# Two transformer blocks on one core: the first stage in half rows, and buffer classes that begin at multiples of 1 KB

## The chip, the cores and the metric

The kernel runs on one core of a Trainium2 chip. The metric is the device time of one execution in microseconds (us). Before the change it is 1069.44 us, the median of three runs (1069.07 to 1070.16).

## The reference

512 rows of 1,024 numbers in fp32 go through two blocks.

- **Block 1.** `h = rms_norm(x, norm_g)`; `proj = h @ w_in`, split into the q, k, v and gate z of a differential attention with four heads, and the q, six k/v streams, gate z and mixing gates of a sparse attention that adds a compressed, a selected and a window branch. `x = x + concat(o_diff, o_nsa) @ w_out`.
- **Block 2.** `h = rms_norm(x, g_mix)`; `proj = h @ w_in_2`, split for a short causal convolution, an attention over the 128 best keys by an index score with a relative bias (`rel_bias`, 32 buckets by 8 heads), and two gates; `x = x + merged @ w_out_2`. Then `x = x + (silu(h2 @ w_ffn_gate) * (h2 @ w_ffn_up)) @ w_ffn_down` with 2,816 inner columns, and a last rms_norm.

Block 1 starts with the function that matters at the start of the kernel:

```python
def rms_norm(x, g):
    xf = x.astype(jnp.float32)
    r = lax.rsqrt(jnp.mean(xf * xf, axis=-1, keepdims=True) + RMS_EPS)
    return (xf * r).astype(x.dtype) * g
```

## The kernel before

**Products.** An fp32 product is made of three fp32r matmuls. Each operand is a pair, hi (the value rounded to fp32r) and lo (the rest), and `mm3` issues hi·hi, hi·lo and lo·hi into one PSUM bank. In each matmul one operand is loaded as weights (the stationary one, 128 x 128) and the other streams past (the moving one, 256 to 512 columns). In the trace's names `acc<-whi,hT` is moving `whi`, stationary `hT`; the last name is the stationary one. Three generators write the dense products: `gen_ii` keeps activations (`hT`) stationary and moves the weights in units of 256 to 320 columns; `gen_i` keeps weights stationary and moves all 512 rows; `gen_tt` moves weights of 512 columns. The gate and up products of the feed-forward part go in pairs by a scheme with seven block products (class `Pair`, L1277 to L1345); their stationary operand is the weight (`wh`, `wl`) and their moving one `hA` with 256 columns.

**Weights.** `_load` (L195) issues the DMA of a unit of weights on SP's queue, `_split` makes the pair: ACT casts (L206, `whi`), DVE or POOL subtracts (L208, `wlo`).

**Buffers.** All tiles in SBUF come from classes of equal buffers that are used in turn: `k8` (13 of 8,192 B per partition), `k4` (13 of 4,096 B), `kf` (3 of 4,096 B), `k2` (19 of 2,048 B), `sm` (28 of 96 B). A constant (`K.const`) is a class of its own. The classes are laid out in the order of their first use. By their sizes, behind a scratch area of 4,096 B that the program has anyway and four constants of 32 B, `kf` and `k4` begin at byte 4,224 (128 beyond a multiple of 1,024) and `k2` at 69,760 (128 beyond one). `mhalf`, `identF`, `sm`, `identR` and `ones` follow with 3,776 B, so that `k8` begins at 112,448 (832 beyond a multiple of 1,024, 320 beyond one of 512). `hT`, `hA`, `act`, `mg`, `qk` and `oTd` stand in `k8`; raw weights, `whi`, `wlo`, `wh` and `wl` in `k4`, with one exception: `split_of` (L1264) puts the pair of weights of some first blocks, `early`, into one `k8` buffer, under the name `wh`.

**The first stage** (L423 to L467, L1452 to L1467). The rows of `x` come as four row tiles of 128, each by two DMAs of 512 columns. Meanwhile `norm_g` is spread over the partitions: eight numbers of each partition's row are transposed (`grow`, `gT`), then broadcast and transposed back into `gB1`, whose first half DVE copies and whose second ACT. TensorE runs 6 transposes of `identF` into `warm` ahead of `grow`, and 12 more are written behind the copies. Then, row tile by row tile, `rms_rows` (L371) squares and sums both halves (ACT; the second half of the first tile DVE, L377), POOL adds and takes the power -0.5 (L383, L384), DVE scales the halves (L385, L389, `xn`), and `put_hT` (L395) transposes each half by four transposes, casts (ACT, `hT` hi) and subtracts (DVE, `hT` lo). After each row tile but the first `K.step()` issues a step of the first dense product, `dk0`. `relative_rows` (L523) loads `rel_bias` transposed into `rbT`; `constants` (L478) loads the small vectors (`gv`, `vrow`, `lmb`).

**The order.** Within an engine the instructions stand in the order of a scheduler that runs over the program with times of its own; so a row in the program may be issued ahead of an earlier one. The queues of DMA are set by the same pass.

## Time and profile before

| what | value |
|---|---|
| median of three runs | 1069.44 us (1069.07 to 1070.16) |
| profiled execution | 1070.19 us, of which the span of the trace is 1068.4 us |
| mean granted clock of TensorE, share of full speed | 0.994 |
| busy time of PE (matmul) | 1043.4 us, 98% of the span, 7,257 instructions |
| busy time of DVE, ACT, POOL | 720.0, 556.2 and 396.8 us |
| DMA | 109.69 MB, mean 103 GB/s |

The profile names TensorE PE, VectorE DVE, ScalarE ACT and GpSimd POOL. The span is what the trace covers; the profiled execution lasted 1.8 us longer than it. A time in the timeline is counted from the start of the span. The end of a matmul is modelled, and matmuls are pipelined, so the time that one more matmul costs is not its duration but the distance from its start to the next start: a row of n matmuls that lasts T has a spacing of (T minus the duration of one) over n minus 1.

### The profile page before, as it was taken

To read this page: it belongs to the slowest core of one execution; us is meant where nothing else is said; L and a number is where in the kernel's file an instruction comes from. 1 tells how busy PE (TensorE), PEld (TensorE's weight loads), DVE (VectorE), ACT (ScalarE), POOL (GpSimd) and SP (SyncE) were. 2 spreads that over 40 slices of the span, in tenths; PEclk is the share of its full clock that TensorE was granted. 3 is DMA by queue.
4 is the path that set the end of the run, shared out by engine and by line. 5 is a ranking of instruction groups with operands and counts; after the bars stand their busy time and mean duration, and the time that the engine had idled before them with its cause. 6 is when DMAs were issued, how large, how long until landed. Compare 5 with 4: busy or idle time off the path is not lost.

```text
span 1068.4 us, 18973 instructions
## 1 busy us (share of the span) xinstructions
PE 1043.4 (98%) x7257; PEld 962.7 (90%) x7257; DVE 720.0 (67%) x1468; ACT 556.2 (52%) x1155; POOL 396.8 (37%) x403
## 2 busy tenths in 40 slices
PE   6999999999999999999999999999999999999997
PEld 6999898899779899888888888989999999999995
DVE  5787467446994646999423653979987777777724
ACT  5476678647884445632323776436544444444433
POOL 3442357466367322112115875920012112121241
PEclk8999999999999999999999999999999999999999
DMA  5344421221114435335322323641433323333122
GB/s 167 114 138 136 102 62 41 58 82 60 57 43 129 140 92 167 100 98 155 112 79 69 90 70 108 237 139 60 158 109 119 117 82 100 94 114 109 31 90 79
DMA packets 128085, 109.69 MB, mean 103 GB/s; under 512 B 20393, under 2 KB 119154, under 8 KB 127994
## 3 DMA queue, kind: packets, MB, share of 16 engines
q1 hardware_dynamic: 126906, 105.83, 32.6%
q0 software_dynamic: 1072, 2.65, 0.7%
q8 instruction: 57, 0.93, 0.4%
q14 instruction: 34, 0.28, 0.1%
q10 hardware_dynamic: 16, 0.00, 0.0%
HBM read 103.13 MB, written 6.84 MB: 103 GB/s over the span
## 4 chain that ended last, share of the span: by engine, by line
PE 90%; DVE 4%; POOL 2%; ACT 2%; issue 1%; DMA 0%; SPq 0%; POOLq 0%; DVEq 0%; ACTq 0%
PE acc L164 76%; PE pt L178 5%; PE sc L164 4%; PE o L164 4%; POOL wlo L208 1%; ACT p L636 1%; DVE p L634 1%; DVE acc L1513 0%; POOL mg L1213 0%; DVE mg L1216 0%; PE warm L178 0%; DMA gv<-in_diff_k_norm_g 0%; ACT junk L380 0%; DVE PTa L653 0%; ACT whi L206 0%
## 5 line engine op out<-in xcount | busy, mean ns | idle before, releaser
L208 POOL TENSOR_TENSOR wlo<-raw,whi 128x1024 fp32r<-128x1024 f32 (+4 forms) x99 | 205.0, 2075 | 444.4 <-ACT whi L206 365.5
L164 PE MATMUL acc<-hA,wh 128*128 128x256 f32 x1264 | 218.0, 279 | 0.7 <-ACT wh L1272 0.7
L206 ACT CAST whi<-raw 128x1024 fp32r<-128x1024 f32 (+4 forms) x143 | 132.0, 924 | 125.1 <-PE acc L164 80.1
L164 PE MATMUL acc<-hT,whi 128*128 128x512 f32 x608 | 194.5, 398 | 0.0
L164 PEld LDWEIGHTS acc<-hA,wh 128*128 128x128 f32 x1264 | 189.0, 189 | 1.3 <-ACT wh L1272 0.9
L164 PE MATMUL acc<-whi,hT 128*128 128x256 f32 (+3 forms) x896 | 180.7, 290 | 1.0 <-DVE hT L402 1.0
L164 PE MATMUL acc<-hA,wl 128*128 128x256 f32 x584 | 162.4, 278 | 0.0
L164 PEld LDWEIGHTS acc<-whi,hT 128*128 128x128 f32 x896 | 144.1, 189 | 1.7 <-DVE hT L402 1.2
L164 PEld LDWEIGHTS acc<-hT,whi 128*128 128x128 f32 x608 | 112.2, 188 | 24.5 <-ACT r L1512 0.2
L164 PE MATMUL acc<-whi,act 128*128 128x256 f32 (+1 forms) x640 | 130.0, 289 | 0.0
L164 PE MATMUL acc<-wlo,hT 128*128 128x256 f32 (+3 forms) x448 | 128.6, 288 | 0.0
L164 PE MATMUL acc<-hT,wlo 128*128 128x512 f32 x304 | 120.9, 398 | 0.0
L164 PEld LDWEIGHTS acc<-hA,wl 128*128 128x128 f32 x584 | 109.6, 188 | 0.0
L164 PEld LDWEIGHTS acc<-whi,act 128*128 128x128 f32 x640 | 103.9, 188 | 2.5
L164 PE MATMUL acc<-wlo,act 128*128 128x256 f32 (+1 forms) x320 | 92.3, 289 | 0.0
L636 ACT ACTIVATE p<-p,s 128x128 f32<-128x128 f32 (+3 forms) x128 | 72.2, 565 | 29.9 <-DVE s L634 27.1
L164 PEld LDWEIGHTS acc<-wlo,hT 128*128 128x128 f32 x448 | 84.4, 189 | 0.4
L1272 ACT CAST wh<-raw 128x1024 fp32r<-128x1024 f32 x55 | 57.6, 1052 | 50.1 <-PE acc L164 43.6
L1273 DVE TENSOR_TENSOR wl<-raw,wh 128x1024 fp32r<-128x1024 f32 x51 | 63.3, 1245 | 29.8 <-PE acc L164 17.3
L208 DVE TENSOR_TENSOR wlo<-raw,whi 128x1024 fp32r<-128x1024 f32 (+5 forms) x44 | 53.6, 1221 | 42.3 <-ACT whi L206 42.2
L164 PEld LDWEIGHTS acc<-hT,wlo 128*128 128x128 f32 x304 | 57.2, 188 | 13.1
L164 PEld LDWEIGHTS acc<-wlo,act 128*128 128x128 f32 x320 | 60.1, 188 | 1.3
(279 smaller groups left out, 2044.4 us busy)
## 6 DMA issues: line engine op xcount, KB each, us to landing
raw<-in_w_in SPq DMA_DIRECT2D x52, 512.0 KB, 3.6
raw<-in_w_ffn_gate SPq DMA_DIRECT2D x28, 512.0 KB, 3.6
raw<-in_w_ffn_up SPq DMA_DIRECT2D x22, 512.0 KB, 4.6
raw<-in_w_ffn_down SPq DMA_DIRECT2D x36, 256.0 KB, 5.2
raw<-in_w_out SPq DMA_DIRECT2D x16, 512.0 KB, 3.3
raw<-in_cmp_w SPq DMA_DIRECT2D x8, 512.0 KB, 3.6
raw<-in_w_in SPq DMA_DIRECT2D x10, 384.0 KB, 3.4
rel_all<-rel_rows POOLq DMA_DIRECT2D x1, 2560.0 KB, 18.0
```

Source lines behind the costliest of these rows:

```text
L164: self.nc.tensor.matmul(out, lhsT, rhs, start=start, stop=stop, skip_group_check=True)
L178: self.nc.tensor.transpose(out, in_, ident)
L206: self.nc.scalar.copy(hi, raw)
L208: (self.nc.gpsimd if every and self.split and self.split % every == 0 else self.nc.vector).tensor_tensor(lo, raw, hi.bitcast(F32), op=OP.s ...
L634: V.tensor_tensor_reduce(out=p[:, :n], in0=sc[:, :n], in1=bias, scale=-scale, scalar=3e38, op0=OP.add, op1=OP.min, accum_out=nm)
L636: S["exp"] = A.activation(p[:, :n], p[:, :n], AF.Exp, scale=-1.0, bias=nm, accum_out=z).ins
L1272: A.copy(hi, src)
L1273: eng.tensor_tensor(lo, src, f32(hi), op=OP.subtract)
```

## The change

- The warming transposes are 6 and 6 in place of 6 and 12, and the last 6 move `gB1` past `identF`, where the 12 moved nothing that anything else writes.
- Six constants (`identF` 512 B, `KC` 256 B, `mhalf`, `ones`, `rowok`, `c01` of 32 B each: 896 B) are made ahead of all else. With the 4,096 B and the four constants of before they make 5,120 B, so that `kf`, `k4` (from 5,120 on), `k2` (70,656) and `k8` (109,568, taken ahead of the other constants since `new_hT()` is called early) all begin at multiples of 1,024 B.
- Both halves of `gB1` are copied by ACT.
- The loop over row tiles is `first_rows`: for each tile the sums (the second half on DVE for the first two tiles), then scaling and transposing of half 0, then scaling of half 1, then transposing of half 1 of the tile before. `K.step()` follows every tile, the first too.
- The DMA of `rbT` is issued after the last one of `x`.

```diff
-WARM = 6, 12
+WARM = 6, 6
...
+    identF, KC = K.const([P, P], "identF"), K.const([P, 64], "KC")
+    mhalf, ones, rowok = [K.const([P, 1], name) for name in ("mhalf", "ones", "rowok")]
+    c01 = K.const([P, 2], "c01")
     xin = [t("kf" if tt < 3 else "k4", [P, D], F32, "xt") for tt in range(NT)]
...
     x_load(0)
-
-    mhalf = K.const([P, 1], "mhalf")
+    S["hT"] = new_hT()
+
     V.memset(mhalf, -0.5)
-    identF = K.const([P, P], "identF")
...
-        copy((V, A)[b], gB1[:, b * T:(b + 1) * T], pt.rearrange("p a b -> p (a b)"))
-    for _ in range(WARM[1]):
-        K.tr(warm, identF, identF)
+        A.copy(gB1[:, b * T:(b + 1) * T], pt.rearrange("p a b -> p (a b)"))
+    for b in range(WARM[1]):
+        K.tr(warm, gB1[:, b * P:(b + 1) * P], identF)
...
-        nc.sync.dma_start(rbT, h["rel_bias_2"].rearrange("b h -> h b"))
+        with tc.issue_after(S["x"]):
+            nc.sync.dma_start(rbT, h["rel_bias_2"].rearrange("b h -> h b"))
...
+    def first_rows():
+
+        rs, xn = {}, {}
+
+        def stats(tt):
+            ss, r = sm(2), sm(1)
+            for c in range(2):
+                a, junk = xin[tt][:, c * T:(c + 1) * T], t("k2", [P, T], F32, "junk")
+                if c and tt < 2:
+                    V.tensor_tensor_reduce(out=junk, in0=a, in1=a, scale=1.0 / 1024.0, scalar=0.0, op0=OP.mult,
+                                           op1=OP.add, accum_out=ss[:, c:c + 1])
+                else:
+                    A.activation(junk, a, AF.Square, scale=1.0 / 32.0, accum_out=ss[:, c:c + 1])
+            G.tensor_scalar(r, ss[:, 0:1], ss[:, 1:2], EPS, op0=OP.add, op1=OP.add)
+            G.tensor_tensor(r, r, mhalf, op=OP.pow)
+            rs[tt] = r
+
+        def norm(tt, b):
+            a = slice(b * T, (b + 1) * T)
+            xn[tt, b] = t("k2", [P, T], F32, "xn")
+            V.scalar_tensor_tensor(xn[tt, b], xin[tt][:, a], rs[tt], gB1[:, a], op0=OP.mult, op1=OP.mult)
+
+        def put(tt, b):
+            pt = ps([P, 4, P], name="pt")
+            for k in range(4):
+                K.tr(pt[:, k, :], xn[tt, b][:, k * P:(k + 1) * P], identF)
+            s = slice(tt * P, (tt + 1) * P)
+            A.copy(S["hT"][0][b][:, :, s], pt)
+            V.tensor_sub(S["hT"][1][b][:, :, s], pt, f32(S["hT"][0][b][:, :, s]))
+            tick()
+
+        for tt in range(NT):
+            stats(tt)
+            norm(tt, 0)
+            put(tt, 0)
+            if tt == 0:
+                K._split()
+            norm(tt, 1)
+            if tt:
+                put(tt - 1, 1)
+            K.step()
+        put(NT - 1, 1)
...
-    for tt in range(NT):
-        halves = [xin[tt][:, 0:T], xin[tt][:, T:D]]
-        xn = rms_rows(halves, gB1, BOTH, tt == 0)
-        if tt == 0:
-            K._split()
-        put_hT(xn, tt, S["hT"])
-        if tt:
-            K.step()
+    first_rows()
```

On PE, at the start of the program, the order before is this (`pt<-identF,s` are the transposes that make `gB1`):

```order
L178 MATMUL warm<-identF 128x128 x18
L178 MATMUL pt<-identF,grow 128x8
L178 MATMUL pt<-identF,s 128x128 x8
L178 MATMUL pt<-identF,xn 128x128 x16
L164 MATMUL acc<-whi,hT 128x256
L164 MATMUL acc<-wlo,hT 128x256
```

and with the change:

```order
L178 MATMUL warm<-identF 128x128 x6
L178 MATMUL pt<-identF,grow 128x8
L178 MATMUL pt<-identF,s 128x128 x8
L178 MATMUL warm<-identF,gB 128x128 x4
L178 MATMUL pt<-identF,xn 128x128 x4
L178 MATMUL warm<-identF,gB 128x128 x2
L164 MATMUL acc<-whi,hT 128x256
L164 MATMUL acc<-wlo,hT 128x256
```

All 18 warming transposes stood ahead of `grow`, also the 12 written behind it; now 6 do, and the first matmul of `dk0` stands behind 4 transposes of `xn` in place of 16 (12 matmuls later there is a row of 16).

On DVE, from the copy of `gT` on, before:

```order
L447 COPY s<-pt 128x8
L377 ISA junk,s<-xt 128x512
L377 ISA s 128x1
L277 COPY gB<-pt 128x512
L385 SCALAR_TENSOR_TENSOR xn<-xt,s,gB 128x512
L389 SCALAR_TENSOR_TENSOR xn<-xt,s,gB 128x512
L402 TENSOR_TENSOR hT<-pt,hT 128x4x128 x2
L208 TENSOR_TENSOR wlo<-raw,whi 128x1024
```

and with the change, up to the last scaling and the `GD` constant (made of `gv`):

```order
L1470 SCALAR_TENSOR_TENSOR xn<-xt,s,gB 128x512 x2
L1478 TENSOR_TENSOR hT<-pt,hT 128x4x128
L1459 ISA junk,s<-xt 128x512
L1459 ISA s 128x1
L208 TENSOR_TENSOR wlo<-raw,whi 128x1024
L1470 SCALAR_TENSOR_TENSOR xn<-xt,s,gB 128x512 x2
L208 TENSOR_TENSOR wlo<-raw,whi 128x1024
L1470 SCALAR_TENSOR_TENSOR xn<-xt,s,gB 128x512 x2
L208 TENSOR_TENSOR wlo<-raw,whi 128x840
L1470 SCALAR_TENSOR_TENSOR xn<-xt,s,gB 128x512 x2
L1478 TENSOR_TENSOR hT<-pt,hT 128x4x128 x6
L504 TENSOR_TENSOR GD<-gv 128x64
```

The copy of `gB` is gone from DVE, one subtraction for `hT` stands ahead of the first `wlo` in place of two, and six of the eight stand in a row behind all scalings.

On SP's queue the first rows before are:

```order
L429 DMA xt<-in_x 128x512 x2
L525 DMA rbT<-in_rel_bias 8x32x1
L195 DMA raw<-in_w_in 128x4x256
L429 DMA xt<-in_x 128x512 x2
L195 DMA raw<-in_w_in 128x4x256
```

and with the change:

```order
L433 DMA xt<-in_x 128x512 x2
L195 DMA raw<-in_w_in 128x4x256
L433 DMA xt<-in_x 128x512 x2
L195 DMA raw<-in_w_in 128x4x256
L433 DMA xt<-in_x 128x512 x4
```

`rbT` has left its place behind the first tile of `x` and stands behind the loads of the first weights and of `cmp_w2`.

## Rows read from the trace of the kernel before

**Rows 1.** The chain that ended last, shares of the span by engine.
```profile
PE 90%; DVE 4%; POOL 2%; ACT 2%; issue 1%; DMA 0%; SPq 0%; POOLq 0%; DVEq 0%; ACTq 0%
```

**Rows 2.** Windows: us, busy PE, PEld, DVE, ACT, POOL, PEclk, DMA share, GB/s.
```profile
5.00:10.00 5.00, 3.29 (x21) 2.77 (x19) 2.88 (x6) 1.02 (x2) 0.88 (x2) 0.84 1.01 358
10.00:15.00 5.00, 0.38 (x2) 0.00 (x0) 2.94 (x4) 4.73 (x11) 1.27 (x2) 0.50 1.09 318
15.00:20.00 5.00, 4.53 (x27) 4.53 (x28) 4.24 (x7) 3.44 (x9) 3.79 (x6) 0.64 0.08 19
```

**Rows 3.** Timeline of PE, first stage: start, us, engine, line, operation, idle before and releaser.
```profile
1.69 3.77 PE L178 MATMUL warm<-identF 128*128 128x128 f32 x18 [1.69 <-POOL identF masks.py:199]
...
8.42 1.97 PE L178 MATMUL pt<-identF,xn 128*128 128x128 f32 x8 [1.46 <-DVE xn L385]
15.47 1.97 PE L178 MATMUL pt<-identF,xn 128*128 128x128 f32 x8 [5.09 <-DVE xn L385]
17.09 0.56 PE L164 MATMUL acc<-whi,hT 128*128 128x256 f32 x1
...
32.39 0.29 PE L164 MATMUL acc<-wlo,hT 128*128 128x280 f32 x1
```

**Rows 4.** Timeline of DVE and ACT, first stage.
```profile
5.65 0.17 DVE L447 COPY s<-pt 128x8 f32<-128x8 f32 x1 [4.11 <-PE pt L178]
5.74 0.68 DVE L377 CUSTOM_DVE_ANT_0 junk<-xt 128x512 f32<-128x512 f32 x1
7.61 0.75 DVE L385 SCALAR_TENSOR_TENSOR xn<-xt,s,gB 128x512 f32<-128x512 f32 x1 [0.36 <-POOL s L384]
12.59 1.22 DVE L208 TENSOR_TENSOR wlo<-raw,whi 128x1024 fp32r<-128x1024 f32 x1 [0.86 <-ACT whi L206]
...
11.53 1.03 ACT L206 CAST whi<-raw 128x1024 fp32r<-128x1024 f32 x1
```

**Rows 5.** Timeline of POOL and DVE around the constant GD, and PE's wait there.
```profile
25.30 2.00 POOL L208 TENSOR_TENSOR wlo<-raw,whi 128x840 fp32r<-128x840 f32 x1 [4.81 <-ACT whi L206]
25.40 1.98 DVE L506 TENSOR_TENSOR GD<-gv 128x64 f32<-128x64 f32 x1 [1.33 <-DMA gv<-in_diff_k_norm_g]
PE acc L164 <- DVE hT L402: 1.0, 1, 1.0
```

**Rows 6.** What the DMA engines moved in each us from 0 to 40.
```profile
GB/s 0 35 307 208 151 268 360 377 390 395 391 369 316 276 238 92 3 0 0 0 3 13 38 31 94 64 40 39 148 288 325 74 0 76 320 129 0 0 16 0
```

**Rows 7.** Timeline of PE: the first feed-forward products, weights and `hA` both in `k8`.
```profile
717.46 5.92 PE L164 MATMUL acc<-hA,wh 128*128 128x256 f32 x48
...
725.32 6.00 PE L164 MATMUL acc<-hA,wh 128*128 128x256 f32 x48
```

**Rows 8.** Timeline of PE: later feed-forward products, weights in `k4`.
```profile
736.06 0.39 PE L164 MATMUL acc<-hA,wh 128*128 128x256 f32 x2
...
740.48 0.39 PE L164 MATMUL acc<-hA,wh 128*128 128x256 f32 x2
...
797.05 0.40 PE L164 MATMUL acc<-hA,wh 128*128 128x256 f32 x2
...
799.53 0.40 PE L164 MATMUL acc<-hA,wh 128*128 128x256 f32 x2
```

**Rows 9.** Windows of PE, matmuls into `acc` alone: us, busy (count), PEclk, DMA.
```profile
756.00:1038.00 282.00, 281.33 (x2427) 1.00 0.32 101
444.90:550.90 106.00, 106.00 (x455) 1.00 0.39 114
```

**Rows 10.** Groups of matmuls by form: count, busy us, mean ns.
```profile
L164 PE MATMUL acc<-hA,wh 128*128 128x256 f32 x1264 | 218.0, 279 | 0.7 <-ACT wh L1272 0.7
L164 PE MATMUL acc<-hT,whi 128*128 128x512 f32 x608 | 194.5, 398 | 0.0
L164 PE MATMUL acc<-hA,wl 128*128 128x256 f32 x584 | 162.4, 278 | 0.0
L164 PE MATMUL acc<-whi,hT 128*128 128x256 f32 x576 | 111.0, 284 | 1.0 <-DVE hT L402 1.0
L164 PE MATMUL acc<-whi,act 128*128 128x256 f32 x576 | 110.3, 278 | 0.0
```

## The prediction

> **What bounds the kernel now.** I read first the chain of waits by engine [rows 1]: 90% of the path is PE, no queue and no DMA has 1%. So a microsecond goes only where PE waits, or where a matmul takes less of PE's time. [...] Last I looked at what one matmul costs in the body [rows 7 to 9], since the second part of the change moves every operand to another address, and the body is 98% of the time.

> **Part 1: the first stage.** Before, the 18 warming transposes all stand ahead of `grow`: 3.77 us, 0.21 us each, from 1.69 on [rows 3]. DVE gets `gT` at 5.65, and behind it stands the sum over the second half of the first tile of x, at 5.74 [rows 4]; its `xn` starts at 7.61, 1.87 us later, the two POOL steps among it. With 12 fewer, `grow` is free at about 1.69 + 6 x 0.21 = 2.95, 2.5 us earlier. The x tile then comes last: its 512 KB are the first in the queue, and the DMA engines had moved 35 + 307 + 208 + 151 = 701 KB by the end of the fifth column [rows 6]. The dip in the fourth and fifth stands where `rbT`, 256 elements of 4 bytes, followed x on the queue; with that moved back I take the second half at 4.2 to 4.7, so DVE starts its sum at about 4.5 and `xn` at 4.5 + 1.87 = 6.4 in place of 7.6: 1.2 us. The DVE copy of `gB` (0.7 us) lies in DVE's wait for POOL, and ACT, which does both now, has nothing else to do until then. The 6 transposes of `gB` wait for these ACT copies; behind them on PE stand only the transposes of `xn`, which need the same `gB`. That costs nothing; if ACT were late, it would cost at most the two copies, 1.2 us, on a path that has slack further on.

> Then half 0 alone is scaled, transposed, cast and subtracted. Before, `dk0`'s first matmul stood behind 16 transposes, the last 8 of which needed the second tile's `xn` (PE waited 5.09 us for it), and began at 17.09 [rows 3]. Now it stands behind 4, and waits for `wlo` of the first weights: before 12.59 + 1.22 = 13.8, since ACT cast `whi` at 11.53 behind two `hT` casts and a sum [rows 4]. Now one cast and one sum stand ahead: I take `whi` from about 9.2 to 10.2, `wlo` to about 11.5. The sum over the second tile's second half stands ahead of `wlo` on DVE and waits for x: x, weights, x are 1.57 MB, moved by 7.7 us [rows 6] plus about 1.5 us to land, as `raw` and x did before. It just fits.

> What ends this stage is DVE's row: behind `wlo` 0 stand 6 scalings at 0.75, a `wlo` at 1.22 and one of 840 columns at 1.0, together 6.7 us, so the last scaling ends near 11.5 + 6.7 = 18.2. In that time PE runs 12 to 16 of `dk0`'s 96 matmuls, partly at the lower clock. From about 18.5 on 80 remain, at 0.118 us each 9.4 us, with 4 transposes (0.5): `dk0` would end at 28.4 to 28.9. Before, its last 256-column matmul stood just ahead of the first 280-column row at 32.39, so at 32.2 [rows 3]. The gain is about **3.5 us**. In it lies the stall at 27 us: POOL's `wlo` and DVE's `GD` ran side by side 2.0 us each, and PE waited 1.0 us for the `hT` behind `GD` [rows 5]; now six of the last seven `hT` stand ahead of `GD`. Bounds: 0, if DVE's row is late by as much (a rival below), and 5.4, if matmuls of the second tile already fill PE in the DVE row. Behind `dk0` PE is the bound, so the gain stays. The moved `rbT` is past six loads of weights and x on SP's queue, 1 KB, used only in block 2's bias: nothing.

> **Part 2: the addresses.** [...] The first feed-forward products have `hA` and their weights both in `k8`: 48 matmuls in 5.92 us, (5.92 - 0.28)/47 = 120.0 ns, and again 121.7 in the second row (its end is modelled) [rows 7]. Later, with the same `hA` but weights in `k4`, 13 triples between 736.06 and 740.48 make 4.42/39 = 113.3 ns; elsewhere 7 triples between 797.05 and 799.53 make 2.48/21 = 118.1 [rows 8]. Over the whole stretch 2,427 matmuls take 281.33 us, 115.9 ns, at PE without gaps [rows 9]. Moving tile, shapes and clock are the same in rows 7 and 8; what differs is the class of the stationary operand. `k4` begins at 128 and `k8` at 320 above a multiple of 512, so in rows 7 the two streams have the same place within 512 B, and in rows 8 they do not. I read 120.0 as the price of two streams in the same place.

> After the change all classes begin at multiples of 1,024, so every pair of operands has that relation. If the relation sets the price:
> - the 2,427 of the stretch go from 115.9 to 120.0: 2,427 x 4.1 ns = **9.9 us**. Bounds 0 and 9.9.
> - the other matmuls of 256 columns. By the groups there are 1,264 + 584 with `hA`, 576 and half as many lo with `act`, the same with `hT` [rows 10], and by the code 448 with `oTd`, `mg` and `At`: 4,024 in all, less 2,427, less the 96 of rows 7: 1,501. I take them from the slower of the two other spacings, 118.1, to 120.0: **2.9 us**. Bounds: 0, and from 113.3 to 120.0, 10.1 us.
> - those of 512 columns: 608 + 304 with `hT` [rows 10] and by the code five products of 96: 1,392. They are at 106.00/455 = 233.0 ns [rows 9]. No row has a long run of them with both operands in one class. Each has one weight load like those of 256, so I take the same 1.9 ns: **2.6 us**. Bounds: 0, and up to 2 x 120.0, 7.0 ns each, 9.7 us.
> - those of 264 to 320 columns and the attention's: nothing taken; they are few.

> Sum: +9.9 + 2.9 + 2.6 = +15.4, less 3.5: +11.9 us. On the profiled execution's 1070.19 that is 1082.1; this execution lies 0.75 above the median, so **1081** against 1069.44.

> That no operand stood at a multiple of 256 before is the weak point: the absolute place is new, and a gain from it has no row that excludes it.

> **The rivals.**
> *Addresses cost nothing.* The spread 113.3 to 120.0 would then come from what runs beside PE, and rows 7 from their neighbours. For it: 113.3 and 118.1 occur with the same classes on both sides [rows 8], so something else moves the spacing too. Against it: 120.0 holds only where classes agree, in both rows 7. It gives the gain of the first stage alone: 1069.4 - 3.5 = 1066. [...]

> *Alignment is the best place.* The other side of the forecast, by one mechanism: operands at multiples of 1 KB never meet, and all matmuls run at the fast spacing of rows 8. Then 2,427 x 2.6 = 6.3, 1,501 x (118.1 - 113.3) = 7.2, 96 x 6.7 = 0.6, and 1,392 x (233.0 - 226.6) = 8.9: 23.0 us, with the start 26.5: 1043; half of it would give 1055. It decides as soon as the feed-forward spacing falls under 115.9. For it: 113.3 exists in long stretches. Against it: the only equal places that a row shows are the slowest.

> *The first stage gains nothing.* DVE's sum of the second x tile holds `wlo` until x lands, and the clock is at its lower level longer, as no warming work stands between 7 and 11 us: matmuls of `dk0` at 0.21 us in place of 0.118 cost 0.09 each, 12 to 40 of them 1.1 to 3.6 us. Then `dk0` ends near 32, and the change with no effect of addresses is at 1069, with the forecast's effect at 1085.

> **How the numbers follow.** About 0.2% of the time, 2.1 us, is what a measurement of this kernel can tell from none. Forecast (1081, own range 1072 to 1090): 0.43. A smaller effect of addresses that only part of the products shows, 1070 to 1075: 0.10. Addresses cost nothing, start gains, 1064 to 1068: 0.22. Alignment is best, 1043 to 1060: 0.20. First stage gains nothing and addresses nothing, 1068 to 1072: 0.05. Faster: 0.20 + three quarters of 0.22 = 0.37. Same: the rest of that 0.22, half of the last, a little of the second: 0.10. Slower: 0.53. The range 1055 to 1090 leaves out the larger half of the alignment gain and the upper bounds of the address terms (up to 1099), together under 2 in 10.

> **What the profile after would show.** For the forecast: feed-forward rows at 120 ns in long x48-like runs, the 756-to-1038 stretch near 291 us for as many matmuls, `dk0`'s end near 28.5, first real matmul near 11.5. If the spacing stays a mixture of 113 and 118, the second part is wrong and the time is 1066; if it is 113 throughout, its sign is wrong. If the 280-column rows begin after 31, the first part is wrong. Both parts can be read apart: the start of that row, and the distance from it to the end.

## The result and the profile after

The changed kernel takes 1076.57 us (median of four runs, 1076.19 to 1078.32) against 1069.39 us: a ratio of 1.0072, 95% interval 1.0059 to 1.0084. It is **7.2 us slower**. The prediction was 1081 us, slower with a chance of 0.53, range 1055 to 1090.

The page of the changed kernel (span, busy time, the chain that ended last, three groups of matmuls) answers to [rows 1, 10]:

```profile
span 1074.4 us, 18962 instructions
...
PE 1052.1 (98%) x7251; PEld 976.4 (91%) x7251; DVE 716.8 (67%) x1469; ACT 555.5 (52%) x1154; POOL 397.4 (37%) x403
...
PE 90%; DVE 5%; ACT 2%; DMA 1%; POOL 1%; issue 1%; SPq 0%; POOLq 0%; DVEq 0%; ACTq 0%
...
L164 PE MATMUL acc<-hA,wh 128*128 128x256 f32 x1264 | 225.4, 283 | 1.4 <-ACT wh L1270 1.4
...
L164 PE MATMUL acc<-hT,whi 128*128 128x512 f32 x608 | 191.3, 393 | 0.0
...
L164 PE MATMUL acc<-hA,wl 128*128 128x256 f32 x584 | 165.1, 283 | 0.0
```

PE is the bound as before. The same 1,264 matmuls of 256 columns take 225.4 us in place of 218.0, while the 608 of 512 columns take 191.3 in place of 194.5. The two shapes moved in opposite directions.

The timeline of PE in the first stage of the changed kernel, beside [rows 3]:

```profile
1.69 1.54 PE L178 MATMUL warm<-identF 128*128 128x128 f32 x6 [1.69 <-POOL identF masks.py:199]
...
6.79 0.65 PE L178 MATMUL pt<-identF,xn 128*128 128x128 f32 x4 [0.40 <-DVE xn L1470]
...
9.67 0.58 PE L164 MATMUL acc<-whi,hT 128*128 128x256 f32 x1 [2.01 <-ACT whi L206]
10.96 0.58 PE L164 MATMUL acc<-wlo,hT 128*128 128x256 f32 x1 [0.70 <-DVE wlo L208]
...
29.47 0.29 PE L164 MATMUL acc<-wlo,hT 128*128 128x280 f32 x1
```

The first matmul starts at 9.67 in place of 17.09, and the 280-column unit behind `dk0` at 29.47 in place of 32.39: the first stage gained 2.9 us.

Windows of PE, matmuls into `acc` alone, first of the kernel before, then of the changed one. 450 to 540 us holds only 512-column matmuls, 770 to 1030 only those of 256:

```profile
450.00:540.00 90.00, 90.00 (x388) 1.00 0.41 120
770.00:1030.00 260.00, 260.00 (x2246) 1.00 0.31 97
```

```profile
450.00:540.00 90.00, 90.00 (x399) 1.00 0.42 120
770.00:1030.00 260.00, 260.00 (x2169) 1.00 0.32 96
```

PE is full in all four and its clock is at 1.00. Time over count gives the spacing (the distance from one matmul's start to the next): 256 columns went from 115.8 to 119.9 ns, 512 columns from 232.0 to 225.6. The counts take in the matmuls that reach over an edge of the window. From start to start, 512 columns went from 233.3 to 226.7, so every spacing of 512 columns below is about 1 ns low, in all kernels alike.

A kernel bound by one engine can be accounted for by landmarks: the start of the first matmul of each kind in the timelines of both profiled executions.

| from, to (first matmul of each) | before, us | after, us | difference |
|---|---|---|---|
| start of the span, 280-column unit | 32.39 | 29.47 | -2.9 |
| to `oTd` (mostly attention, 256 columns) | 282.25 | 283.26 | +1.0 |
| to `oTn` (256 columns) | 29.46 | 30.02 | +0.6 |
| to `yc` (mostly 512 columns) | 207.24 | 205.62 | -1.6 |
| to `mg` (512 columns) | 118.57 | 116.58 | -2.0 |
| to `hA` (both) | 47.55 | 47.61 | +0.1 |
| to `act` (256 columns, two waits) | 49.17 | 50.75 | +1.6 |
| to `act` with 512 columns (256 columns alone) | 272.66 | 282.24 | +9.6 |
| to the end of the span | 29.11 | 28.85 | -0.3 |
| sum | 1068.4 | 1074.4 | +6.0 |

These are the profiled executions, 0.8 us above its kernel's median before and 0.4 under it after; so the sum is 6.0 and not 7.2. Within the fourth row stands a loss that has nothing to do with matmuls: PE waits 1.5 us for a tile `bV` that it did not wait for before (last section).

### The profile page after: what moved, and what is told of

It is laid out like the page before. It is cut to its first block, busy times and chain, and to the rows that moved or that the text cites. A ratio compares the mean times of both kernels' runs of the same rounds, so it can differ in the third digit from the quotient of the medians.

```text
span 1074.4 us, 18962 instructions
## 1 busy us (share of the span) xinstructions
PE 1052.1 (98%) x7251; PEld 976.4 (91%) x7251; DVE 716.8 (67%) x1469; ACT 555.5 (52%) x1154; POOL 397.4 (37%) x403
## 3 DMA queue, kind: packets, MB, share of 16 engines
q0 software_dynamic: 1072, 2.65, 0.6%
## 4 chain that ended last, share of the span: by engine, by line
PE 90%; DVE 5%; ACT 2%; DMA 1%; POOL 1%; issue 1%; SPq 0%; POOLq 0%; DVEq 0%; ACTq 0%
PE acc L164 77%; PE pt L178 5%; PE sc L164 4%; PE o L164 4%; DMA raw<-in_w_in 1%; ACT p L635 1%; DVE p L633 1%; DVE acc L1547 0%; DVE mg L1214 0%; DVE hA L1399 0%; DMA raw<-in_w_out 0%; DVE PTa L652 0%; ACT PTa L651 0%; POOL p L1021 0%; DVE sum L1313 0%
## 5 line engine op out<-in xcount | busy, mean ns | idle before, releaser
L164 PE MATMUL acc<-hA,wh 128*128 128x256 f32 x1264 | 225.4, 283 | 1.4 <-ACT wh L1270 1.4
L164 PEld LDWEIGHTS acc<-hA,wh 128*128 128x128 f32 x1264 | 193.9, 192 | 2.0 <-ACT wh L1270 1.6
L164 PE MATMUL acc<-hT,whi 128*128 128x512 f32 x608 | 191.3, 393 | 0.0
L164 PE MATMUL acc<-whi,hT 128*128 128x256 f32 (+3 forms) x896 | 183.5, 293 | 2.1 <-ACT whi L206 2.0
L164 PE MATMUL acc<-hA,wl 128*128 128x256 f32 x584 | 165.1, 283 | 0.0
L164 PEld LDWEIGHTS acc<-whi,hT 128*128 128x128 f32 x896 | 146.3, 191 | 3.3 <-ACT whi L206 2.3
L164 PE MATMUL acc<-whi,act 128*128 128x256 f32 (+1 forms) x640 | 133.4, 294 | 0.0
L164 PEld LDWEIGHTS acc<-hA,wl 128*128 128x128 f32 x584 | 112.0, 192 | 0.0
L164 PEld LDWEIGHTS acc<-whi,act 128*128 128x128 f32 x640 | 106.3, 192 | 2.5
```

Source lines behind the costliest of these rows:

```text
L164: self.nc.tensor.matmul(out, lhsT, rhs, start=start, stop=stop, skip_group_check=True)
```

## The experiments

Theory A: the addresses cost what was lost, and the first stage gains about 3 us. Theory B: the addresses do nothing. Below, distance is the place of `k8` less the place of `k4` and `k2` (which always agree), modulo 256 B. In the change it is 0; in the kernel before it is 192 (64 less 128).

**Either part alone.**

```diff
 # layout_only: the kernel before
+    identF, KC = K.const([P, P], "identF"), K.const([P, 64], "KC")
+    mhalf, ones, rowok = [K.const([P, 1], name) for name in ("mhalf", "ones", "rowok")]
+    c01 = K.const([P, 2], "c01")
     xin = [...]
...
     x_load(0)
+    S["hT"] = new_hT()
...
 # rows_only: the changed kernel, these lines taken out again, each constant where it stood before
```

> The kernel before with the constants placed first and nothing else: all classes at multiples of 1,024 B, the first stage and the order of every engine as before. Theory A (the addresses cost, the new first stage gains 2.9 us, the time by which dk0 ends earlier in the changed kernel): 1076.6 + 2.9 = 1079.5 us, all 256-column matmuls at 120.0 ns, those of 512 columns near 227 ns. Theory B (the addresses do nothing, the first stage or the order lost the time): 1069.4 us and a mixture of 113 and 118 ns.

> The changed kernel with the constants back in their old places (kf, k4 and k2 at 128 above a multiple of 1,024, k8 at 832), so the new first stage alone. Theory A: 1069.4 - 2.9 = 1066.5 us, 256 columns at 113 to 118 ns, 512 columns near 233 ns. Theory B: 1076.6 us.

layout_only took 1078.83 us, 1.0091 (1.0076 to 1.0106) of the kernel before, whose order of instructions it has on every engine. Theory B falls: **moving the buffers, with nothing else changed, costs 9 us**. Not all of it is slower matmuls. Of the 9.6 us by which its profiled execution is longer, 1.5 are the wait on `bV`, which other kernels with other addresses have too (last section). Another 1.6 stand behind that wait: from `oTn` to `yc` layout_only takes 207.2 us where the changed kernel, with the same wait, takes 205.6, and its granted clock is down there (windows of PE; the changed kernel has 1.00 in both):

```profile
440.00:450.00 10.00, 6.11 (x23) 0.89 0.20 54
450.00:460.00 10.00, 10.00 (x43) 0.94 0.34 87
```

That leaves 6.5 us for the slower matmuls; the changed kernel's rows give the same sum (9.6 + 2.3 - 5.4, below).

rows_only took 1069.44, 1.0003 (0.9993 to 1.0013): its matmuls are back at the old spacings (from `act` to `act` with 512 columns 272.65 us, before 272.66), but the expected 1066.5 did not come. The 280-column unit starts at 29.05 and the first product with `hA` at 714.12, both 3.3 us ahead of before; at the first use of `act` the lead is 0.8. What lies between is, in rows_only, one wait of PE, and two windows of PE behind it:

```profile
PE acc L164 <- ACT wh L1274: 1.8, 1, 1.8
```

```profile
760.00:764.00 4.00, 3.12 (x18) 0.78 1.08 361
764.00:768.00 4.00, 4.00 (x30) 0.79 0.05 16
```

The kernel before waited 0.7 us for `wh`, at clock 1.00. So PE waits 1.1 us longer, and behind the wait its granted clock averages 0.78 and 0.79 in the two windows; from 762.71 to 765.27 us twelve matmuls start 0.21 us apart. PE is busy for 7.12 of the 8 us, and at a mean of 0.785 I estimate the loss at 7.12 x 0.215 = 1.5 us. Together 2.6, less 0.2 from another wait: 2.4 of the lost lead of 2.5. In the new program the scheduler gave this part another order on PE, ACT and DVE; on ACT two casts of `wh` stand ahead of a copy of `part` that they stood behind. Which of these changes lengthens the wait, no run separates.

**Is it that order?** One line gives the feed-forward part its old order on every engine (the first step of `dk0` is issued after the second row tile, as before):

```diff
-            K.step()
+            if tt:
+                K.step()
```

> rows_only (the new first stage on the old addresses) with the one edit of k8_plus64_ffn_order: dk0's first step after the second row tile, which gives the feed-forward part the order of the kernel before. Theory C (the first stage gains 3.3 us on the chip, and rows_only came out level with the kernel before only since PE waits there 1.8 us for wh in place of 0.7 and its clock falls for some us behind that wait): the wait goes back to about 0.7, no window between 756 and 768 us has a granted clock under 1.00, and the time is 1069.5 - 3 = about 1066.7. Rival (what rows_only lost lies elsewhere, or this edit costs the first stage its gain): 1069.4.

1067.07 us, 0.9981 (0.9972 to 0.9990). Its wait for `wh`, and its window of PE from 756 to 768 us:

```profile
PE acc L164 <- ACT wh L1274: 0.7, 1, 0.7
```

```profile
756.00:768.00 12.00, 11.34 (x95) 1.00 0.47 155
```

The wait is back at 0.7, the clock is at 1.00, and the lead of 3.1 us at `hA` (714.35 against 717.46) is 3.3 at the end of the span (1065.1 against 1068.4). Theory C holds: the first stage is worth 3 us in the traces (2.2 by the medians, 1069.30 against 1067.07), and an order that changed 700 us later took them back.

**What in the address counts?** The changed kernel with a constant of n bytes ahead of `k8`:

```diff
+    pad = K.const([P, n // 4], "pad")
     S["hT"] = new_hT()
```

> The changed kernel with 64 B more of constants ahead of k8: k8 at 64 above a multiple of 1,024, kf, k4 and k2 at 0. Theory A1 (what counts is that both operands of a matmul have the same place within 512 B): 256 columns back to a mixture of 113 to 118 ns, 512 columns to 233 ns, about 1066.5 us. Theory A2 (what counts is that the stationary or the moving operand itself stands at a multiple of 1,024 B): the weights still do, so products with weights in k4 keep their 120.0 ns for 256 columns, and the time stays near 1076.

> The changed kernel with 256 B more ahead of k8: k8 at 256 above a multiple of 512 and of 1,024, kf, k4 and k2 at 0. Theory A1 with a period of 512 B: 113 to 118 ns for 256 columns, 233 ns for 512 columns, about 1066.5 us. A1 with a period of 256 B or less: no difference to the changed kernel, 120.0 and 227 ns, 1076.6 us. Theory A2: near 1076.

> The changed kernel with 32 B more ahead of k8 (k8 at 32, all other classes at 0 above a multiple of 256). Theory A1, now with a period of 256 B and the distance of the two operands' places as what counts: a distance of 32 is a new place; if the steady 120.0 ns for 256 columns belongs to distance 0 alone, these are again at 113 to 118 ns and the time is near 1064.7; if it reaches over neighbouring places (a span of 64 B), 120.0 ns and 1076.6 us.

> As k8_plus32 with 96 B. A1: 256 columns at 113 to 118 ns, 512 columns between 227 and 234 ns, time between 1062 and 1068. If the price grows evenly with the distance from 0, it is better than 64 B, which gave 1064.7; if 64 B is a best place of its own, worse.

> As k8_plus32 with 128 B, half of the period: both directions (weights moving past activations, activations past weights) have the same distance. A1: no 120.0 ns, 256 columns at 113 to 118 ns; with an even growth of the price's fall it is the best of all, near 1060; with a period of 128 B it is the changed kernel's 1076.6.

> The changed kernel with 192 B more ahead of k8: kf, k4 and k2 at 0, k8 at 192 above a multiple of 256. This is the distance of the kernel before (k4 at 128, k8 at 64 above a multiple of 256: also 192), at other places. Theory A1 (the distance modulo 256 decides): the same spacings as rows_only: 256 columns at a mean of 115.5 to 116.7 ns, 512 columns of hT at 233.5 ns, time 1069.4 within 1.5. Theory A2 (the place of each operand decides): something else, as 32, 96 and 128 B gave 118 to 120 ns.

The same two windows as above in k8_plus64, then k8_plus96, then k8_plus192:

```profile
450.00:540.00 90.00, 90.00 (x395) 1.00 0.42 120
770.00:1030.00 260.00, 260.00 (x2247) 1.00 0.33 99
```

```profile
450.00:540.00 90.00, 90.00 (x388) 1.00 0.42 120
770.00:1030.00 260.00, 260.00 (x2180) 1.00 0.31 95
```

```profile
450.00:540.00 90.00, 90.00 (x387) 1.00 0.40 114
770.00:1030.00 260.00, 260.00 (x2246) 1.00 0.32 97
```

All layouts with the new first stage, by window time over count (a few records can be missing, so the last digit of a spacing is loose). The 512 columns are products that move activations past weights. Of the 256 columns about two thirds do so (`hA`), and a third moves weights past activations (`act`):

| kernel | distance | 256 columns, ns | 512 columns, ns | time, us |
|---|---|---|---|---|
| changed | 0 | 119.9 | 225.6 | 1076.57 |
| k8_plus256 | 0 | 119.9 | 226.1 | 1076.68 |
| k8_plus32 | 32 | 117.3 | 232.0 | 1076.05 |
| k8_plus64 | 64 | 115.7 | 227.8 | 1064.67 |
| k8_plus96 | 96 | 119.3 | 232.0 | 1080.07 |
| k8_plus128 | 128 | 118.6 | 232.0 | 1077.57 |
| k8_plus192 | 192 | 115.8 | 232.6 | 1067.99 |
| rows_only_ffn_order (old places) | 192 | 115.7 | 232.6 | 1067.07 |

Theory A2 falls at k8_plus64: the weights stand at multiples of 1 KB as in the change, and 115.7 stands in place of 119.9. k8_plus256 (119.9 and 226.1, at 0 119.9 and 225.6) agrees with a period of 256 B or a part of it, and k8_plus128 (118.6 and 232.0) not with one of 128. k8_plus192 and the old places have the same distance at other addresses, and the same spacings (115.8 and 115.7, 232.6 and 232.6): what counts in these layouts is the distance, not the address. Every kernel holds a check of this: the first 96 feed-forward products have both operands in `k8` [rows 7], distance 0 wherever `k8` stands, and the first row of 48 takes 5.91 or 5.92 us (120 ns each) in k8_plus32, 64, 96, 128 and 192, as in the kernel before. In k8_plus64:

```profile
709.40 5.91 PE L164 MATMUL acc<-hA,wh 128*128 128x256 f32 x48
```

Three of my expectations missed. I took 120 ns to belong to distance 0 alone and the price to fall evenly. 32 gives 117.3 ns, but 1076.05 us and not the 1064.7 that I had named for such a spacing; of the 8 us between it and k8_plus192, 3.6 lie between `act` and `act` with 512 columns. 96 gives 119.3 and 1080.07, worse than the change, and 128 is no best place. Only 64 and 192 are good for 256 columns (115.7 and 115.8, the others 117.3 to 119.9). For 512 columns that move activations 0 and 64 are good (225.6 and 227.8, the others 232.0 to 232.6). So 64 is good for both, and k8_plus64 beats the kernel before: 0.9959 (0.9944 to 0.9974).

The distance has a direction. Where weights move past activations it is the other way round, and 64 becomes 192. The last 512-column matmuls, with `act`, are such; their second and their last, 94 spacings apart, in the kernel before, then in k8_plus64:

```profile
1039.29 0.39 PE L164 MATMUL acc<-wlo,act 128*128 128x512 f32 x1
...
1060.81 0.40 PE L164 MATMUL acc<-whi,act 128*128 128x512 f32 x1
```

```profile
1032.37 0.40 PE L164 MATMUL acc<-wlo,act 128*128 128x512 f32 x1
...
1054.30 0.40 PE L164 MATMUL acc<-whi,act 128*128 128x512 f32 x1
```

They take 21.52 us (228.9 ns each) before and 21.93 (233.3) in k8_plus64: here the old places, with 64 seen from the moving operand, are the better ones.

Nor does the distance settle a spacing alone. The same 175 matmuls with `mg`, in k8_plus64 and then, with the same addresses, in k8_plus64_ffn_order (below):

```profile
664.16 0.39 PE L164 MATMUL acc<-whi,mg 128*128 128x256 f32 x1 [0.70 <-DVE mg L1215]
...
684.00 0.50 PE L164 MATMUL acc<-whi,mg 128*128 128x256 f32 x2
```

```profile
665.45 0.38 PE L164 MATMUL acc<-whi,mg 128*128 128x256 f32 x1 [0.70 <-DVE mg L1215]
...
686.04 0.51 PE L164 MATMUL acc<-whi,mg 128*128 128x256 f32 x2
```

19.84 us against 20.59, some 4 ns each, as between the two stretches of [rows 8]. So the table's values are means over faster and slower stretches. What chooses between these, and why the price has this shape, no run shows.

**The better version, and the parts of the first stage.** k8_plus64 with the edit of the feed-forward order; from it, 18 warming transposes ahead of `grow`, or `rbT` back behind the first tile of x:

```diff
-WARM = 6, 6
+WARM = 18, 6
```

```diff
-        with tc.issue_after(S["x"]):
-            nc.sync.dma_start(rbT, ...)
+        nc.sync.dma_start(rbT, ...)
```

> k8_plus64 with one edit more: the first step of dk0 is issued after the second row tile, as in the kernel before, which gives the feed-forward part the order that it has in the kernel before (the casts of wh on ACT stood otherwise in the changed kernel, and PE waits there 1.4 to 1.8 us for wh in place of 0.2 to 0.7). Theory C (the new first stage's gain of 3 us is partly given back by that order): from the first feed-forward product to the first use of act about 1 us less than in k8_plus64, and the time near 1063.7 if the first stage is not slower for it. Rival (the order costs nothing, PE's waits there only move): 1064.7, and later by what the first stage loses.

> k8_plus64_ffn_order with 18 warming transposes ahead of grow, as they stood in the kernel before, in place of 6. Theory D (these transposes hold the chain that sets the end of dk0): gT comes 2.4 us later, xn of the first tile 1.6 us later, dk0's end about 1.5 us later, and the time is 1063.35 + 1.5 = 1064.9. Rival (DVE's row of scalings and wlo sets the end of dk0 and has slack ahead of it, or the longer warming keeps the clock up and gives back what it costs): 1063.4 or under.

> k8_plus64_ffn_order with the DMA of rbT back in its place behind the first tile of x. Theory: the second half of that tile lands about 0.5 us later (the sum over it starts on DVE near 4.6 in place of 4.1), xn and dk0's end with it: 1063.9. Rival: the tile does not wait for rbT, or DVE's row has slack: 1063.4.

k8_plus64_ffn_order took 1063.35 us, 0.9942 (0.9925 to 0.9959), **6.2 us under its kernel before and 13 under the change**. The stretch from `hA` to `act` fell from 50.5 to 49.3 us, the expected 1 us; the profiled execution lost 1.5 us elsewhere, on `bV`.

ffn_order_18_warm took 1064.08 us. Its timeline of PE, then of DVE:

```profile
1.69 4.10 PE L178 MATMUL warm<-identF 128*128 128x128 f32 x18 [1.69 <-POOL identF masks.py:199]
...
14.17 1.97 PE L178 MATMUL pt<-identF,xn 128*128 128x128 f32 x8 [4.73 <-DVE xn L1471]
...
31.05 0.29 PE L164 MATMUL acc<-wlo,hT 128*128 128x280 f32 x1
```

```profile
6.02 0.17 DVE L451 COPY s<-pt 128x8 f32<-128x8 f32 x1 [4.47 <-PE pt L178]
...
7.97 1.41 DVE L1471 SCALAR_TENSOR_TENSOR xn<-xt,s,gB 128x512 f32<-128x512 f32 x2 [1.18 <-POOL s L1465]
```

`gT` comes 2.5 us later than with six, `xn` 2.0 later, and the 280-column unit starts at 31.05 in place of 28.93, so theory D holds for the stage: 2.1 us. At the end only 0.7 is left, since this kernel escapes the 1.5 us on `bV`. The medians of the two kernels are too near each other to say more; the loss was read in the traces.

ffn_order_rbT_early took 1062.59 us, no slower than the kernel that it comes from. The sum over the second half of the first tile, in it and in k8_plus64_ffn_order:

```profile
4.04 0.69 DVE L1460 CUSTOM_DVE_ANT_0 junk<-xt 128x512 f32<-128x512 f32 x1 [0.40 <-DMA xt<-in_x]
```

```profile
4.07 0.69 DVE L1460 CUSTOM_DVE_ANT_0 junk<-xt 128x512 f32<-128x512 f32 x1 [0.43 <-DMA xt<-in_x]
```

It starts at the same time: the tile does not wait for `rbT`. The theory falls: the move of `rbT` gained nothing here.

## Why the prediction was right, and where its steps were not

**Feed-forward stretch: right.** Predicted +9.9 us from 115.9 to 120.0 ns; measured +9.6, at 119.9. One pair of rows, 48 matmuls each, with both operands in one class [rows 7], carried the whole forecast, and layout_only with k8_plus64 shows that the reading (the distance of the operands, not their neighbours in time) was right. The granted clock was 1.00 in the stretches of [rows 7] and of [rows 8] alike. Two things beside it were not known. The relation was taken modulo 512 B, and k8_plus256 agrees with 256 or a part of it, which changed nothing here. And other distances are not free of the price (119.3 ns at 96): that the old places stood at 192, one of the two best, was the old layout's luck, and the forecast rested on its measured 115.9.

**The other 256-column matmuls: right in size.** Predicted +2.9; the second, third and seventh rows of the landmark table, which hold most of them, give +1.0, +0.6 and +1.6. Of the last only 0.7 is the addresses' (layout_only, with the old order, takes 49.9 us there in place of 49.2); the rest is the order of the feed-forward part (below). So +2.3.

**512 columns: the failed step.** I charged 1.9 ns each, +2.6 us, by analogy with 256 columns, with bounds from 0 to +9.7. Those that move activations became 6 ns faster (232.0 to 225.6), those with `act` that move weights 2 ns: the two rows from `oTn` to `mg` and the last row give -1.6 - 2.0 - 0.3, and -1.5 more without the wait on `bV`: about -5.4 us. The bound from below should have been open, as the text itself said of the absolute place. With no row of a long 512-column run at this distance, a gain had not been excluded. These 8.0 us are more than the whole miss: the forecast's +11.9 on the profiled execution came out as +6.0, since the wait on `bV`, the order and a smaller gain of the first stage took back 1.5, 0.9 and 0.6. That 1076.57 lies near 1081 is in part such offsetting.

**First stage: right in sum, mixed in its terms.** Predicted -3.5, measured -2.9 in the change and -3.3 on the old addresses, where the matmuls of 256 columns are shorter (in `dk0` 118 ns apart before, 120 in the change). `xn` came at 6.0 (predicted 6.4), `wlo` ended at 10.9 (11.5), DVE's last scaling at 18.4 (18.2). The first matmul of `dk0` did not wait for `wlo`, as the prediction has it, but for `whi`, and came at 9.67 in place of 11.5; the `wlo` matmuls came at 10.96. The lower clock that the prediction counts with is the 0.50 of [rows 2]; at that clock the kernel before starts `dk0`'s matmuls 0.21 us apart (17.45 to 18.09), and so does the changed kernel (nine from 11.34 to 13.26, granted clock 0.50 from 10 to 16 us). The term for `rbT` was zero: the dip in [rows 6] did not delay the tile.

**Not foreseen:** the wait on `bV` (+1.5), and the order of the feed-forward part, which costs 2.5 us on the old addresses and, by the wait for `wh` (1.4 us against 0.2 in layout_only), 0.9 us on the new ones. I looked at the order only where the first stage stood.

**The rivals.** "Addresses cost nothing" is shown wrong by layout_only (119.9 ns for 256 columns by the same windows, before 115.8); by the distance between its two operands alone TensorE's spacing goes from 115.7 ns (k8_plus64) to 119.9 (the change). "Alignment is the best place" was wrong for 256 columns and right for 512. "The first stage gains nothing" fell with the 280-column unit at 29.47.

## What to carry to other kernels

When one engine is full for the whole span, compute the spacing of its instructions for every pair of buffer classes before and after any change of layout; an edit that adds or moves a small constant ahead of big classes can be worth more than the edit that it belongs to (here about 6.5 us, against 2.9 of the first stage). Do not choose a round alignment unmeasured: vary the distance between the classes of the two matmul operands in steps of 32 B over 256 B and read the spacings of each shape. Where a scheduler sets the order, compare the whole order, not the stage that was rewritten, and account by landmarks.

## What the runs showed of the hardware

```profile
441.07 2.87 DVE L1547 SCALAR_TENSOR_TENSOR acc<-r,iws,acc 128x512 f32<-128x512 f32 x1
443.86 0.34 DVE L1167 TENSOR_TENSOR bV<-acc,bV 128x64 fp32r<-128x64 f32 x2
...
441.01 2.38 POOL L208 TENSOR_TENSOR wlo<-raw,whi 128x1024 fp32r<-128x1024 f32 x1 [10.60 <-PE acc L164]
```

```profile
PE pt L178 <- DVE bV L1167: 1.5, 1, 1.5
```

```profile
442.58 0.75 DVE L1513 SCALAR_TENSOR_TENSOR acc<-r,iws,acc 128x512 f32<-128x512 f32 x1
...
442.67 2.92 POOL L208 TENSOR_TENSOR wlo<-raw,whi 128x1024 fp32r<-128x1024 f32 x1 [10.73 <-DVE qs L1161]
```

  In these rows the one that started second took longer. In the changed kernel that is DVE's, with 2.87 us, which takes 0.75 in the kernel before; `bV` stands behind it and comes late, and PE waits 1.5 us. In the kernel before it is POOL's, with 2.92 us, which takes 2.38 in the changed one, and PE does not wait. The 1.5 us came and went between kernels without any edit near it: the changed kernel, layout_only, k8_plus256, k8_plus64_ffn_order and ffn_order_rbT_early have it, the others not.
